# Feature products of 512 tokens run as two halves of 256, and one place for the memory key weights

## The chip, the cores and the metric

One core of one Trainium2 chip runs the whole kernel. The metric is the device time of one launch in microseconds (us), median of the runs shown; lower is better.

## What is computed

A decoder trunk of two layers over 512 tokens of width 1024, in float32. Each layer has three sub-layers, each between two RMS norms and added to the residual `x`:

```
x = x + rmsnorm(hybrid_mixer(rmsnorm(x)))            # one input projection; 8 heads of dilated causal
                                                      # attention, 4 mLSTM heads with a causal conv on
                                                      # q and k; one output projection
x = x + rmsnorm(memory_cross_attention(rmsnorm(x), mem))   # 4 heads, 256 memory tokens
x = x + rmsnorm(conv_ffn(rmsnorm(x)))                 # gated MLP of width 2816, conv of width 3
```

The change touches projections only: of the mixer, the conv inputs qm and km (`h @ w_in`, eight column blocks of 128) and attention's q and k (four and four blocks); of the cross attention, the queries (`h @ wq`) and the memory keys (`mem @ wk`).

## The kernel before, in words

**Products in three parts.** Every operand of a large product is split into a float32r high part and a float32r rest (`split`, L101: a copy on ScalarE, a subtraction on VectorE). `mm3` (L116) then issues three matmuls for one product: high by high, high by rest, rest by high. Weights come from DRAM as units of 128 x 1024 (512 KB), one `raw` tile each, and are split into a `whi` and a `wlo` tile. Such a tile is 1152 columns wide and the 1024 columns of weights start in it at an offset (`w_tiles`, L89): `offs` is the pair of offsets of `whi` and `wlo`, `WOFF` is (16, 48).

**Two kinds of product.** A *feature* product (`feat_gen`, L173) makes 128 features of all 512 tokens: the weights are stationary, the activations move. One unit is 8 blocks of the contraction by 3 matmuls, 24 matmuls of 512 columns, summed in one PSUM bank; after each block the generator yields. A *token* product (`tok_gen`, L203) has the activations stationary. `feat_halves` (L184) is a feature product that goes over tokens 0 to 255 for several units before tokens 256 to 511; it serves the first four query units of the cross attention and the first four units of the MLP, always at `WOFF`.

**Where `feat_gen` is used**, per layer: eight units U_Q and U_K of attention (L745, L746, at `WOFF`), eight conv units U_QM and U_KM (L722, each with its own pair out of `OFFS`), the last four of the eight query units of the cross attention (L1021, at `WOFF`), and `fill_k` (L423), which makes the memory keys: eight units per layer of 256 columns (the 256 memory tokens), at `OFFS[m]`; the first four of layer 1 are made earlier, in layer 0, at `WOFF`. That is 20 units of 512 columns per layer, 40 in all.

**The order of work.** TensorE's order is written out by the program: `run` (L154) takes one step of the main generator and then calls `tick` (L128), which lets side tasks that are due issue their matmuls. Due times come from a planned clock, `now`, which `mm` (L107) moves on for each matmul by a cost, and from waits in `PACE`. While the mixer's feature units run, the side tasks are the attention groups (scores, transposes of the probabilities `s`, products with the values) and the gates. So TensorE's stream there is a run of feature matmuls, some side matmuls, a run of feature matmuls, and so on; a run is three matmuls or a multiple of three. The other engines and the DMA queue take their instructions in the order that the tile framework plans, except in stretches marked as written by hand.

In the trace the tiles are named by what they are: `B` holds the normalised activations, `mem` the memory tokens, `pg` and `pa` are PSUM. A matmul reads out<-moving,stationary.

Of the kernel before, what the change touches and what calls it, by code (L numbers as in the profile page):

```python
# [21 lines left out]
NM = 256  # L22
# [6 lines left out]
U_QM, U_KM, U_VM, U_V, U_Q, U_K, U_OM = 0, 4, 8, 12, 16, 20, 24  # L29
U_WOUT, U_WQ, U_WK, U_WV, U_WO, U_UP, U_DOWN = 28, 36, 44, 52, 60, 68, 112  # L30
# [8 lines left out]
def trunk_kernel(ctx: ExitStack, tc: tile.TileContext, x4, memt, w, gw, gains, mcw, fcw, gb,  # L39
# [11 lines left out]
    def nm(s):  # L51
        uid[0] += 1
        return f"{s}_{uid[0]}"

    def pg():
        return ps.tile([128, 512], F32, tag="g", name=nm("pg"), bufs=4)
# [41 lines left out]
    def load_unit(l, i, offs=(0, 0)):  # L98
        return w_split(load_raw(l, i), offs)
# [7 lines left out]
    def mm(o, lhs, rhs, **kw):  # L107
        n = math.prod(o.shape[1:])
        now[0] += 0.0025 + (max(0.218, n / 600) if rhs.dtype == F32 else max(0.107, n / 2400))
        PE.matmul(o, lhs, rhs, **kw)  # L110
# [5 lines left out]
    def mm3(o, lh, ll, rh, rl, start, stop, **kw):  # L116
        mm(o, lh, rh, start=start, stop=False, **kw)
        mm(o, lh, rl, start=False, stop=False, **kw)
        mm(o, ll, rh, start=False, stop=stop, **kw)
# [53 lines left out]
    def feat_gen(l, u, act, done, n=512, w=None, offs=WOFF):  # L173
        hi, lo = w or load_unit(l, u, offs)
        acc = pg()
        for k in range(8):
            c = slice(128 * k, 128 * k + 128)
            rh, rl = act(k)
            mm3(acc[:, :n], hi[:, c], lo[:, c], rh, rl, k == 0, k == 7)
            if k == 7:  # L180
                done(acc)
            yield

    def feat_halves(l, units, act, dones, between, after=()):  # L184
        ws = [load_unit(l, u, WOFF) for u in units]
# [140 lines left out]
    def act_of(xn):  # L326
        def f(k):
            return xn[k // 4][:, k % 4, :], xn[2 + k // 4][:, k % 4, :]
        return f
# [86 lines left out]
    def dkv(l, which):  # L416
        if (l, which) not in kv_dram:
            kv_dram[l, which] = dr.tile([128, 2, 1024], F32, name=f"d{which}{l}")
        return kv_dram[l, which]

    OFFS = [(0, 0), (96, 0), (16, 48), (48, 48), (64, 0), (32, 64), (112, 16), (80, 112)]

    def fill_k(act, l, ms, offs=None):  # L423
        dst = dkv(l, "k")
        for m in ms:
            def done(acc):
                kf = pp.tile([128, NM], F32, tag="xg", name=nm("kf"), bufs=PACE["xg"])
                ACT.copy(kf, acc[:, :NM])
                SP.dma_start(dst[:, m // 4, NM * (m % 4):NM * (m % 4) + NM], kf)

            n = 0
            for _ in feat_gen(l, U_WK + m, act, done, NM, offs=offs or OFFS[m]):
                n += 1
                if n % 2 == 0:
                    yield
# [64 lines left out]
    def mixer(l, xn, pend):  # L500
        act = act_of(xn)
# [7 lines left out]
        def m16(tag):  # L509
            return mp.tile([128, 16], F32, tag=tag, name=nm(tag))  # L510
# [4 lines left out]
        cc, inter, floor, wt = m16("cc"), m16("inter"), m16("floor"), m16("wt")  # L515
# [196 lines left out]
        def conv_done(m):  # L712
            def f(acc):
                u = pp.tile([128, 512], F32, tag="xg", name=nm("u"), bufs=PACE["xg"])
                ACT.activation(u, acc, AF.Identity, bias=cw_t[:, m, 4:5], scale=cw_t[:, m, 3:4])
                for j in range(1, 4):
                    DVE.scalar_tensor_tensor(u[:, j:], acc[:, :512 - j], cw_t[:, m, 3 - j:4 - j], u[:, j:],
                                             ALU.mult, ALU.add)
                ACT.activation((qm if m < 4 else km)[:, m % 4, :], u, AF.Silu)
            return f  # L720

        conv = iter([feat_gen(l, U_QM + m, act, conv_done(m), offs=OFFS[m]) for m in range(8)])  # L722

        atasks = []
        for j in range(4):
            qas = [ap.tile([128, 512], F32R, tag=f"qa{i}", name=nm("qa"), bufs=2) for i in range(2)]
            khs = [ap.tile([128, 512], F32R, tag=f"kh{i}", name=nm("kh")) for i in range(2)]

            def q_done(acc, first=8 * (4 * l + j - 1)):
                until(lambda: live.get("S", 0) >= first)  # L730
                for hh in range(2):
                    a, b = hv[hh], hv[1 - hh]
                    ACT.activation(qas[hh][a], acc[a], AF.Copy, scale=0.125)
                    DVE.scalar_tensor_tensor(qas[hh][b], acc[a], 0.125, qas[hh][a].bitcast(F32),
                                             ALU.mult, ALU.subtract)

            def k_done(acc, first=8 * (4 * l + j)):
                until(lambda: live.get("S", 0) >= first)
                for hh in range(2):
                    a, b = hv[hh], hv[1 - hh]  # L740
                    ACT.copy(khs[hh][a], acc[a])
                    ACT.copy(khs[hh][b], acc[a])
                    DVE.tensor_sub(kls[hh][a], acc[a], khs[hh][a].bitcast(F32))

            run(feat_gen(l, U_Q + j, act, q_done))  # L745
            run(feat_gen(l, U_K + j, act, k_done))  # L746
            atasks.append(spawn(att_pair(j, qas, khs), PACE["aw"][l]))
            for _ in range(PACE["cv"][l][j]):
                run(next(conv))
# [514 lines left out]

    for l in range(L):
        mix_close, mixed = mixer(l, xn, pend)
        tail = Tail(l, G_POST_MIX, (l, G_PRE_MEM), PACE[f"nmem{l}"])

# [5 lines left out]
        pend = tail.tasks  # L1274
        xn = tail.xn
        run(fill_k(mem_tiles(pool_mem(tail.tp)), l, range(PACE["kf"][0] if l else 0, 8)))
        tail.close()
        es, tasks, o_t = cross(l, xn, pend)
# [11 lines left out]
        if l == 0:  # L1290
            run(fill_k(mem_tiles(lambda: tail.forms.wide(F32R)), 1, range(PACE["kf"][0]), WOFF))
            tail.forms.free = True
# [91 lines left out]
```

## Time and profile before

| | us |
|---|---|
| median of 3 runs (1556.23 to 1558.34) | 1556.98 |
| the profiled execution's own time | 1557.76 |
| its span, first to last instruction | 1555.9 |
| TensorE matmul busy | 1529.4 (98%) |
| VectorE busy | 1074.2 (69%) |
| ScalarE busy | 892.8 (57%) |

How to read it: busy time of a matmul record is its time from start to modelled end, and records of neighbouring matmuls overlap. What a matmul costs the stream is the step from its start to the start of the next one. In the timeline, neighbouring matmuls of one kind stand in one line with their number, so the step is read between the starts of lines.

### The profile page before, as it was taken

To read this page: it belongs to the slowest core of one execution; us is meant where nothing else is said; L and a number is where in the kernel's file an instruction comes from. 1 tells how busy PE (TensorE), PEld (TensorE's weight loads), DVE (VectorE), ACT (ScalarE), POOL (GpSimd) and SP (SyncE) were. 2 spreads that over 40 slices of the span, in tenths; PEclk is the share of its full clock that TensorE was granted. 3 is DMA by queue.
4 is the path that set the end of the run, shared out by engine and by line. 5 is a ranking of instruction groups with operands and counts; after the bars stand their busy time and mean duration, and the time that the engine had idled before them with its cause. 6 is when DMAs were issued, how large, how long until landed. Compare 5 with 4: busy or idle time off the path is not lost.

```text
span 1555.9 us, 24501 instructions
## 1 busy us (share of the span) xinstructions
PE 1529.4 (98%) x9480; PEld 1350.9 (87%) x9480; DVE 1074.2 (69%) x1808; ACT 892.8 (57%) x1578; POOL 355.7 (23%) x292
## 2 busy tenths in 40 slices
PE   7999999999999999999999999999999999999998
PEld 5788888898899999988887888888988899999886
DVE  5687646746588899963376876557565988998433
ACT  5687574545466666652256875745454666666321
POOL 0000110100026777700010001101000367773000
PEclk9999999999999999999999999999999999999999
DMA  5422245463242333342323222454521233332331
GB/s 179 129 81 79 79 134 166 128 198 110 80 138 82 109 109 109 111 131 98 108 89 115 89 68 82 141 156 142 179 73 35 104 104 112 111 115 91 128 101 55
DMA packets 55430, 173.13 MB, mean 111 GB/s; under 512 B 6801, under 2 KB 9617, under 8 KB 55314
## 3 DMA queue, kind: packets, MB, share of 16 engines
q1 hardware_dynamic: 55314, 171.57, 33.9%
q8 instruction: 74, 1.21, 0.3%
q14 instruction: 42, 0.34, 0.1%
HBM read 165.22 MB, written 6.33 MB: 110 GB/s over the span
## 4 chain that ended last, share of the span: by engine, by line
PE 70%; DVE 15%; ACT 4%; DMA 4%; issue 3%; POOL 2%; SPq 0%; POOLq 0%; DVEq 0%; ACTq 0%
PE pg L110 47%; PE pa L110 21%; DVE wlo L1137 4%; DVE u L1042 4%; PE pa L114 3%; DMA raw<-in_w_dram 2%; DVE wlo L103 2%; ACT u L1037 1%; ACT whi L102 1%; POOL sm L236 1%; DVE xg L262 1%; ACT junk L241 1%; DMA raw<-in_memt_dram 1%; DVE B L1056 1%; DVE x L375 1%
## 5 line engine op out<-in xcount | busy, mean ns | idle before, releaser
L110 PE MATMUL pg<-B,whi 128*128 128x256 f32 (+1 forms) x1800 | 412.4, 323 | 5.6 <-DVE u L1042 4.2
L103 DVE TENSOR_TENSOR wlo<-raw,whi 128x1024 fp32r<-128x1024 f32 x188 | 231.3, 1232 | 215.7 <-ACT whi L102 212.9
L102 ACT CAST whi<-raw 128x1024 fp32r<-128x1024 f32 x188 | 197.1, 1049 | 219.6 <-PE pg L110 136.5
L110 PEld LDWEIGHTS pg<-B,whi 128*128 128x128 f32 x1800 | 286.9, 188 | 25.7 <-ACT b L1131 2.3
L110 PE MATMUL pg<-whi,B 128*128 128x512 f32 x896 | 297.9, 399 | 0.0
L110 PE MATMUL pg<-B,wlo 128*128 128x256 f32 (+1 forms) x896 | 285.8, 319 | 0.0
L110 PEld LDWEIGHTS pg<-whi,B 128*128 128x128 f32 x896 | 168.8, 189 | 35.0 <-DVE B L103 1.3
L236 POOL TENSOR_TENSOR sm<-sm,mhalf 128x1 f32<-128x1 f32 x56 | 34.3, 612 | 719.4 <-DVE sm L361 542.7
L110 PEld LDWEIGHTS pg<-B,wlo 128*128 128x128 f32 x896 | 168.2, 188 | 14.2
L110 PE MATMUL pg<-wlo,B 128*128 128x512 f32 x448 | 175.3, 391 | 0.6 <-DVE sm L254 0.6
L110 PE MATMUL pa<-S,whi 128*128 128x256 f32 x960 | 168.5, 277 | 0.0
L1042 DVE SCALAR_TENSOR_TENSOR u<-pg,fcw,u 128x511 f32<-128x511 f32 (+1 forms) x176 | 131.3, 747 | 37.9 <-ACT u L1037 34.9
L110 PEld LDWEIGHTS pa<-S,whi 128*128 128x128 f32 x960 | 145.7, 189 | 0.0
L1137 DVE TENSOR_TENSOR wlo<-T,whi 128x1024 fp32r<-128x1024 f32 x80 | 131.7, 1646 | 2.5 <-ACT whi L1131 2.3
L110 PE MATMUL pa<-S,wlo 128*128 128x256 f32 x480 | 133.1, 277 | 0.0
L110 PE MATMUL pa<-whi,S 128*128 128x512 f32 x320 | 105.9, 390 | 0.0
L110 PE MATMUL pg<-whi,S 128*128 128x512 f32 x320 | 105.4, 390 | 0.0
L1037 ACT ACTIVATE u<-pg,fcw 128x512 f32<-128x512 f32 x88 | 68.6, 779 | 55.4 <-DVE pg L1185 28.6
L110 PEld LDWEIGHTS pg<-wlo,B 128*128 128x128 f32 x448 | 84.7, 189 | 15.9 <-DVE wlo L103 1.0
L1131 ACT CAST whi<-T 128x1024 fp32r<-128x1024 f32 x80 | 83.9, 1048 | 25.0 <-PE pg L110 10.9
L1137 POOL TENSOR_TENSOR b<-rg,b 128x512 fp32r<-128x512 f32 x40 | 74.0, 1851 | 100.7 <-ACT b L1131 100.7
L110 PEld LDWEIGHTS pa<-S,wlo 128*128 128x128 f32 x480 | 90.8, 189 | 0.0
(264 smaller groups left out, 2944.5 us busy)
## 6 DMA issues: line engine op xcount, KB each, us to landing
raw<-in_w_dram SPq DMA_DIRECT2D x228, 512.0 KB, 3.5
rg<-in_w_dram SPq DMA_DIRECT2D x40, 512.0 KB, 3.5
gain<-in_gains_dram SPq DMA_DIRECT2D x11, 512.0 KB, 4.3
raw<-in_memt_dram SPq DMA_DIRECT2D x20, 256.0 KB, 3.2
tb<-tb_d SPq DMA_DIRECT2D x16, 256.0 KB, 3.6
x<-in_x_dram SPq DMA_DIRECT2D x8, 256.0 KB, 5.4
e<-nmu_d SPq DMA_DIRECT2D x8, 256.0 KB, 3.6
dv<-vf SPq DMA_DIRECT2D x8, 256.0 KB, 4.2
```

What stands on the lines that cost most here:

```text
L102: ACT.copy(hi, src)
L103: DVE.tensor_sub(lo, src, hi.bitcast(F32))
L110: PE.matmul(o, lhs, rhs, **kw)
L114: PE.transpose(o, src, idn)
L236: POOL.tensor_tensor(r, v, mhalf[:, :1], ALU.pow)
L241: ACT.activation(junk[:, :src.shape[-1]], src, AF.Square, accum_out=s_)
L262: DVE.scalar_tensor_tensor(xg, xt[:, c], r, g[h], ALU.mult, ALU.mult)
L375: DVE.scalar_tensor_tensor(xs[t][:, cc], self.hg[hh, t], r, xs[t][:, cc], ALU.mult, ALU.add)
L1037: ACT.activation(u, acc, AF.Identity, bias=fcw_t[:, m, 3:4], scale=fcw_t[:, m, 2:3])
L1042: DVE.scalar_tensor_tensor(u[:, q:], acc[:, :512 - q], fcw_t[:, m, 2 - q:3 - q], u[:, q:], ALU.mult, ALU.add)
L1131: ACT.copy(ws[j, kind][0], source(j, kind))
L1137: sub(ws[j, kind][1], source(j, kind), ws[j, kind][0].bitcast(F32), ALU.subtract)
```

## The change

`feat_gen` works through the tokens 256 at a time: for 512 tokens the eight blocks of the contraction are issued for the first 256 columns and then again for the second 256, 48 matmuls of 256 columns in place of 24 of 512. It yields after every second block, so after six matmuls of 256 where it yielded after three of 512. For 256 columns (`fill_k`) the order is as it was. The table `OFFS` goes; the conv units take the default `WOFF`, and `fill_k` takes (32, 64) for all of its units that had an entry of the table.

```diff
     def feat_gen(l, u, act, done, n=512, w=None, offs=WOFF):
         hi, lo = w or load_unit(l, u, offs)
         acc = pg()
-        for k in range(8):
-            c = slice(128 * k, 128 * k + 128)
-            rh, rl = act(k)
-            mm3(acc[:, :n], hi[:, c], lo[:, c], rh, rl, k == 0, k == 7)
-            if k == 7:
-                done(acc)
-            yield
+        for c0 in range(0, n, 256):
+            cc = slice(c0, c0 + 256)
+            for k in range(8):
+                c = slice(128 * k, 128 * k + 128)
+                rh, rl = act(k)
+                mm3(acc[:, cc], hi[:, c], lo[:, c], rh[:, cc], rl[:, cc], k == 0, k == 7)
+                if k == 7 and c0 + 256 == n:
+                    done(acc)
+                if n == 256 or k % 2:
+                    yield
...
-    OFFS = [(0, 0), (96, 0), (16, 48), (48, 48), (64, 0), (32, 64), (112, 16), (80, 112)]
-
     def fill_k(act, l, ms, offs=None):
...
-            for _ in feat_gen(l, U_WK + m, act, done, NM, offs=offs or OFFS[m]):
+            for _ in feat_gen(l, U_WK + m, act, done, NM, offs=offs or (32, 64)):
...
-        conv = iter([feat_gen(l, U_QM + m, act, conv_done(m), offs=OFFS[m]) for m in range(8)])
+        conv = iter([feat_gen(l, U_QM + m, act, conv_done(m)) for m in range(8)])
```

## Rows read from the trace of the kernel before

**Rows 1.** The profile's page: span, busy time of TensorE, chain by engine

```profile
span 1555.9 us, 24501 instructions
...
PE 1529.4 (98%) x9480; PEld 1350.9 (87%) x9480; DVE 1074.2 (69%) x1808; ACT 892.8 (57%) x1578; POOL 355.7 (23%) x292
...
PE 70%; DVE 15%; ACT 4%; DMA 4%; issue 3%; POOL 2%; SPq 0%; POOLq 0%; DVEq 0%; ACTq 0%
```

**Rows 2.** Busy time in stretches, the mixers' feature units: stretch, length, busy by engine

```profile
core 0: us, PE busy (x) PEld busy (x) DVE busy (x) ACT busy (x) POOL busy (x), PEclk, DMA share, GB/s
...
45.00:166.00 121.00, 121.00 (x635) 100.40 (x634) 95.66 (x253) 90.81 (x178) 2.59 (x2) 1.00 0.29 92
...
822.20:944.00 121.80, 121.80 (x643) 101.34 (x642) 96.30 (x253) 93.31 (x180) 2.58 (x2) 1.00 0.27 87
```

**Rows 3.** Groups by shape, TensorE, 45 to 166 us: the feature matmuls

```profile
L110 PE MATMUL pg<-B,whi 128*128 128x512 f32 x256 | 83.5, 407 | 0.0
L110 PE MATMUL pg<-B,wlo 128*128 128x512 f32 x128 | 50.5, 395 | 0.0
```

**Rows 4.** Timeline, TensorE: start, length, what; 512 columns after transposes

```profile
91.69 0.71 PE L110 MATMUL pg<-B,whi 128*128 128x512 f32 x2
...
92.47 0.63 PE L110 MATMUL pg<-B,whi 128*128 128x512 f32 x2
...
93.17 0.62 PE L110 MATMUL pg<-B,whi 128*128 128x512 f32 x2
```

**Rows 5.** Timeline, TensorE: 256 columns after transposes (first MLP units)

```profile
454.54 0.48 PE L110 MATMUL pg<-B,whi 128*128 128x256 f32 x2
...
455.33 0.40 PE L110 MATMUL pg<-B,whi 128*128 128x256 f32 x2
...
456.03 0.39 PE L110 MATMUL pg<-B,whi 128*128 128x256 f32 x2
...
456.71 0.39 PE L110 MATMUL pg<-B,whi 128*128 128x256 f32 x2
```

**Rows 6.** Timeline, TensorE: 512 columns after score matmuls of 384 columns

```profile
77.83 0.63 PE L110 MATMUL pg<-B,whi 128*128 128x512 f32 x2
...
78.52 0.63 PE L110 MATMUL pg<-B,whi 128*128 128x512 f32 x2
```

**Rows 7.** Timeline, TensorE: 256 columns after token matmuls of 512 columns

```profile
1204.68 0.40 PE L110 MATMUL pg<-B,whi 128*128 128x256 f32 x2
...
1205.38 0.39 PE L110 MATMUL pg<-B,whi 128*128 128x256 f32 x2
...
1206.06 0.39 PE L110 MATMUL pg<-B,whi 128*128 128x256 f32 x2
```

**Rows 8.** Timeline, TensorE: 512 columns after score matmuls of 128 columns

```profile
75.79 0.67 PE L110 MATMUL pg<-B,whi 128*128 128x512 f32 x2
...
76.53 0.63 PE L110 MATMUL pg<-B,whi 128*128 128x512 f32 x2
```

**Rows 9.** Timeline, TensorE: a long run of 512 columns, from a unit's first rest weights

```profile
57.56 0.40 PE L110 MATMUL pg<-B,wlo 128*128 128x512 f32 x1
57.80 0.62 PE L110 MATMUL pg<-B,whi 128*128 128x512 f32 x2
...
58.48 0.62 PE L110 MATMUL pg<-B,whi 128*128 128x512 f32 x2
```

**Rows 10.** Timeline, TensorE: starts of memory key units 2, 3, 5, 6 and 7, layer 0

```profile
303.28 0.40 PE L110 MATMUL pg<-mem,whi 128*128 128x256 f32 x2
...
306.14 0.41 PE L110 MATMUL pg<-mem,whi 128*128 128x256 f32 x2
...
313.21 0.40 PE L110 MATMUL pg<-mem,whi 128*128 128x256 f32 x2
...
315.95 0.39 PE L110 MATMUL pg<-mem,whi 128*128 128x256 f32 x2
...
318.79 0.40 PE L110 MATMUL pg<-mem,whi 128*128 128x256 f32 x2
```

**Rows 11.** Timeline, TensorE: transposes within the memory keys, idle before them in brackets

```profile
308.05 0.63 PE L114 MATMUL pa<-ident,xg 128*128 128x128 f32 x4 [0.31 <-DVE xg L262]
```

**Rows 12.** Timeline, VectorE: the rest weights of the unit of rows 9

```profile
52.63 1.23 DVE L103 TENSOR_TENSOR wlo<-raw,whi 128x1024 fp32r<-128x1024 f32 x1 [1.07 <-ACT whi L102]
```

## The prediction

> **What bounds the kernel now.** I read the page first: TensorE is busy for 1529.4 of 1555.9 us and carries 70% of the chain that ended last [rows 1]. Then the table of stretches, for the two places where most of the changed units run: in 45 to 166 us TensorE is busy for 121.00 of 121.00, in layer 1 for 121.80 of 121.80 [rows 2]. No engine and no transfer is waited for there, so what counts is the step from one matmul's start to the next one's. Busy time does not tell it: the groups by shape give 407 ns for one of the 256 + 128 feature matmuls of that stretch [rows 3], but their records overlap. So I went to the timeline and read starts. A product of three matmuls of 512 columns (a triple, one yield of the generator) steps by 0.70 us in the middle of a run [rows 4, 6]; six matmuls of 256 columns (the same work after the change) step by 0.70 at first and by 0.68 later on [rows 5, 7].
>
> That "later on" is what the forecast hangs on. A run of halves comes to 0.68 only after six to twelve matmuls: 0.79, 0.70, 0.68 after transposes [rows 5], 0.70, 0.68 after wide matmuls [rows 7]. A run of wholes gets there too, but far later: 0.68 shows after more than 30 matmuls without a break [rows 9]. In the mixer the runs are short. I counted them in the timeline of 45 to 166 us: 384 feature matmuls in 67 runs. 30 runs begin after transposes or other small matmuls (23 of one triple, 3 of two, 3 of three, one of 17); 17 begin after side matmuls of 128 columns (5, 9 and 3 of one, two and three triples); 20 after wide ones (8 of one, 6 of two, 4 of three, one of four, one of five). More than half are over after one triple.
>
> **The change part by part.** *Halves in the mixers*, 16 units per layer, 128 triples. Price of a triple, halves against whole:
> - First triple after transposes: 0.79 against 0.78 [rows 4, 5]; the rows are rounded to 0.01, I take +0.015 each, 30 times: +0.45 us.
> - First triple after 128-column matmuls: whole 0.74 [rows 8]; no row shows halves there. Bounds are the row after transposes (+0.015) and the row after wide matmuls (about 0); it is nearer to the first, since both start late (0.74 and 0.78 against 0.69). I take +0.01, 17 times: +0.15.
> - First triple after wide matmuls: 0.70 [rows 7] against 0.69 [rows 6], +0.005, 20 times: +0.1.
> - Second triple of the two late kinds: 0.70 against 0.70 [rows 4, 5], nothing, 19 times.
> - All later ones, and the second after wide matmuls: 0.68 [rows 5, 7] against 0.69 to 0.70 [rows 4, 6], -0.015. That is 21 after wide matmuls, 3 of the 128-column kind, and 18 of the transposes' kind, of which the last five or so gain nothing as the long run has settled by itself [rows 9]: 37 times -0.015, -0.55.
>
> Sum: about +0.2 per mixer, +0.4 for both. The bounds: all halves at 0.68 from the first on would give -1.5 per mixer, none ever at 0.68 would give +2.3 (below).
>
> *Halves of the queries*, four units per layer in the cross attention: 64 triples in 13 runs of two to eight triples, all after wide matmuls. 51 of them are not the first of their run: 51 times -0.015, -0.7.
>
> *One offset for the memory keys.* In layer 0 the unit with (32, 64) runs from 313.21 to 315.95, 2.74 us; its neighbour with (112, 16) takes 2.84, and unit 2, at (16, 48), 2.86 [rows 10]. Ten units get (32, 64) that had another pair. Five have no transposes in between: 5 x 0.11. In five the runs are broken and only the later part gains, half of it: 5 x 0.05. Together -0.8. The row, then, says that the place of the stationary tile counts. The Trainium skill ("TensorE: Matmul & The Clock Gate", section "Step-by-step: what each phase is for") says that weight loads and the moving operand have independent read ports, so that loading the next weights takes no read bandwidth from the running matmul; by it the place would count for nothing and this -0.8 would be 0.
>
> *The conv units' offsets.* All sixteen go to (16, 48). For 512 columns the rows of these units look like those of q and k at (16, 48); no cost. For halves (16, 48) with tile `B` is what rows 5 and 7 show.
>
> *What a wait takes back.* In layer 0's memory keys TensorE waits 0.31 us for a norm on VectorE [rows 11]; the units before it get about 0.25 shorter, and that wait longer by as much. A little more goes the same way in the cross attention: +0.3 in all.
>
> *Edits at nothing.* DMAs, splits, PSUM tiles and evacuations are the same in number, and an evacuation still comes after a unit's last matmul. The rest weights are needed after two halves, not two wholes, 0.23 us earlier; VectorE has them ready at 53.86 for a use at 57.56 [rows 9, 12], and without that cover TensorE would wait 0.2 us at most per unit. Yields come after the same work. The planned clock books 0.219 for two halves where it booked 0.216, 0.08 us per unit, so some side tasks come one yield (0.7 us) earlier among the feature matmuls; with no idle time in the stretch [rows 2] most producers must be well ahead, and I allow 1 us either way for this and for a new order on the other engines.
>
> Sum: +0.4 - 0.7 - 0.8 + 0.3 = -0.8 us. Against the profiled execution's own 1557.76 (span 1555.9) that is 1557.0; that execution lies 0.8 above the median of the runs, 1556.98, so I forecast **1556.2**. A measurement of this kernel tells about 0.2%, 3.1 us, from no change.
>
> **Rivals.** *Settled at once.* If the halves in the mixer run at 0.68 from their second triple on at the latest and lose nothing at the start, every triple gains up to 0.015 save the long run's last: -1.5 per mixer, -3.0 - 0.7 - 0.8 + 0.3 = -4.2, **1552.8**. For it: after wide matmuls the second triple is at 0.68 already [rows 7]. Against: after transposes it is not [rows 5], and those are the most frequent starts.
>
> *Never settled* (slower). The rate after a break has a cause that the mixer renews, and halves stay at what unit 2 of the memory keys shows with the same offsets (16, 48) and another moving tile: 2.86 / 4 = 0.715 for six [rows 10] against 0.695. That is +0.018 for 128 triples, +2.3 per mixer: +4.6 - 0.7 - 0.8 + 0.3 = +3.4, **1560.4**. It decides from about 0.713 for six halves, taken over all. For it: side matmuls break the runs 67 times per mixer. Against: with `B` as moving tile every long run in the trace settled.
>
> *The offset does nothing.* Unit 5 is fast for another reason and the memory keys gain nothing; the waits take back less: +0.4 - 0.7 + 0.1 = -0.2, **1556.8**. For it speaks the rule of the read ports. Against: unit 6, right behind unit 5 in the same quiet stretch, is slow [rows 10].
>
> **How the numbers follow.** Forecast 0.55, own range 1555 to 1558.5 (1 us for the order, and bounds of the 128-column starts); settled at once 0.17; never settled 0.16; offset does nothing 0.12. Faster by over 0.2% (below 1553.9): 0.15 of the second case, some of the first: 0.21. Slower (above 1560.1): most of the third and a little of the first: 0.19. Within: 0.60. The range reaches to both outer cases, 1552.8 to 1560.4, since leaving out both would leave out a third.
>
> **What would show it.** Right: in the mixers' feature units, timeline steps of about 0.79, 0.70, 0.68 for groups of six halves after transposes, and the two stretches (121.0 and 121.8 us) within 1 us of before; the four query units of a layer shorter by 0.35; each quiet memory key unit at 2.74; no idle time of TensorE in the mixers' stretch. Wrong: steps of 0.68 right after transposes (settled at once) or 0.71 throughout (never settled); memory key units still at 2.84; or TensorE idle before transposes of `s`, which would say that the new order cost more than the steps.

## The result and the profile after

The changed kernel takes **1565.43 us** (median of 4 runs, 1562.81 to 1568.26) against 1556.61 for the kernel before on the same chip (4 runs, 1556.00 to 1558.34): a ratio of **1.0059**, 95% interval 1.0047 to 1.0072. It is slower by 0.6%, outside the forecast's range of 1555 to 1558.5 and above its slowest rival, 1560.4. Measured again later it took 1563.80 (5 runs, 1561.74 to 1567.82) against 1555.57, a ratio of 1.0055 [1.0042, 1.0067].

The profiled execution is the fastest of the four: 1562.81 us with a span of 1561.0, against 1557.76 and 1555.9 before. So the two traces show 5.1 of the 8.8 us between the medians. The page, where [rows 1] stood before:

```profile
span 1561.0 us, 26418 instructions
...
PE 1527.9 (98%) x10440; PEld 1394.2 (89%) x10440; DVE 1075.5 (69%) x1808; ACT 894.1 (57%) x1578; POOL 355.4 (23%) x292
...
PE 69%; DVE 16%; ACT 5%; DMA 4%; issue 3%; POOL 2%; SPq 0%; POOLq 0%; DVEq 0%; ACTq 0%
```

TensorE is busy 1.5 us less than before, in a span that is 5.1 longer. The page alone doesn't say where; starts of the same instruction in both traces do. The table gives the time between such starts (the last gate matmul, the first `ones,sq`, the first `mem,whi`, the last `mem,whi`, the first `ph,v` of each layer), read from the timelines. The last `mem,whi` comes 0.2 to 0.6 us ahead of the first query unit; it stands for that unit's start in this table and wherever the stretch to the heads is given below:

| stretch | before | after | difference |
|---|---|---|---|
| start to the mixer's feature units, layer 0 | 45.2 | 45.6 | +0.4 |
| feature units of mixer 0, to its norm | 127.8 | 129.9 | **+2.1** |
| memory keys, layer 0 | 24.6 | 23.5 | -1.15 |
| first query unit to the heads, layer 0 | 50.9 | 53.5 | **+2.6** |
| heads to the mixer's feature units, layer 1 | 449.8 | 449.0 | -0.8 |
| feature units of mixer 1, to its norm | 127.8 | 130.4 | **+2.6** |
| memory keys, layer 1 | 12.8 | 12.6 | -0.2 |
| first query unit to the heads, layer 1 | 50.6 | 50.0 | -0.7 |
| heads of layer 1 to the end | 419.8 | 419.9 | +0.1 |

(The stretches left out, between a mixer's norm and the memory keys, differ by under 0.1.) Three stretches lose 7.3 us. The mixers have idle time now. The busy time of the same lengths as in [rows 2], shifted by 0.6 and 3.1 us, about as late as its units start:

```profile
core 0: us, PE busy (x) PEld busy (x) DVE busy (x) ACT busy (x) POOL busy (x), PEclk, DMA share, GB/s
45.60:166.60 121.00, 119.20 (x1001) 116.72 (x1000) 94.47 (x251) 89.53 (x176) 2.58 (x2) 1.00 0.30 91
825.30:947.10 121.80, 120.20 (x1005) 117.73 (x1004) 95.55 (x251) 90.90 (x177) 2.59 (x2) 1.00 0.30 88
```

TensorE idles 121.00 - 119.20 = 1.8 us and 121.80 - 120.20 = 1.6 us, where [rows 2] had none. Its waits in the first of these stretches (engine, line, what it waited for: us in total, times, longest); the same view of the kernel before is empty:

```profile
engine line waited for: us in total, times, longest us
PE pa L110 <- DVE pl L103: 1.3, 3, 0.6
PE pa L110 <- ACT ph L102: 0.3, 1, 0.3
PE pa L114 <- DVE s L660: 0.2, 1, 0.2
```

These are side tasks of the attention, not the feature tiles that the change touches. Two of the waits in the timeline of TensorE, and what VectorE did before the second one:

```profile
97.23 0.28 PE L110 MATMUL pa<-pl,B 128*128 128x128 f32 x1
97.80 0.39 PE L110 MATMUL pa<-ph,B 128*128 128x256 f32 x1 [0.30 <-ACT ph L102]
...
121.56 0.39 PE L110 MATMUL pa<-pl,B 128*128 128x256 f32 x1 [0.60 <-DVE pl L103]
```

```profile
119.53 0.74 DVE L718 SCALAR_TENSOR_TENSOR u<-pg,mcw,u 128x509 f32<-128x509 f32 x1
120.30 0.69 DVE L703 TENSOR_TENSOR ao<-pa,lo 64x512 f32<-64x512 f32 x1
121.02 0.16 DVE L659 RECIPROCAL sm<-sm 128x1 f32<-128x1 f32 x1
121.09 0.41 DVE L103 TENSOR_TENSOR pl<-pa,ph 128x256 fp32r<-128x256 f32 x1
```

VectorE is not idle: `pl` stands behind the conv's sums `u` and an evacuation. The same product and its `pl` before:

```profile
121.06 0.28 PE L110 MATMUL pa<-pl,B 128*128 128x256 f32 x1
```

```profile
119.36 0.42 DVE L103 TENSOR_TENSOR pl<-pa,ph 128x256 fp32r<-128x256 f32 x1
```

There `pl` was ready 121.06 - 119.36 - 0.42 = 1.28 us ahead. Counted from the last gate matmul (45.20 before, 45.59 after), TensorE now comes to this product 0.5 us earlier (75.37 us, its wait taken off, against 75.86), and VectorE, whose own order has changed too, makes `pl` 1.3 us later (75.50 against 74.16). Together that is 1.8 us: the margin is gone and some 0.55 us are missing, the wait of 0.60.

The feature matmuls themselves do what the forecast said. A run of halves after transposes, to be read against [rows 4, 5]:

```profile
94.80 0.48 PE L110 MATMUL pg<-B,whi 128*128 128x256 f32 x2
...
95.58 0.39 PE L110 MATMUL pg<-B,whi 128*128 128x256 f32 x2
...
96.26 0.39 PE L110 MATMUL pg<-B,whi 128*128 128x256 f32 x2
...
96.94 0.28 PE L110 MATMUL pa<-ph,B 128*128 128x256 f32 x1
```

Six halves take 0.78, 0.68 and 0.68 us (the last line begins the next product). The memory keys, where [rows 10] stood, start at even distances of 2.72 us, and the transposes between them no longer wait [rows 11]:

```profile
309.80 0.60 PE L114 MATMUL pa<-ident,xg 128*128 128x128 f32 x4
...
314.82 0.39 PE L110 MATMUL pg<-mem,whi 128*128 128x256 f32 x2
...
317.54 0.39 PE L110 MATMUL pg<-mem,whi 128*128 128x256 f32 x2
...
320.26 0.39 PE L110 MATMUL pg<-mem,whi 128*128 128x256 f32 x2
```

The third loss is in the cross attention of layer 0. TensorE's waits from 323 to 377 us; before, in the same place, the only one was 1.0 us for `p`:

```profile
PE pa L114 <- DVE p L966: 2.8, 1, 2.8
PE pg L110 <- DVE wlo L103: 0.5, 1, 0.5
```

VectorE's timeline there, with the wait that it causes on TensorE:

```profile
364.26 1.23 DVE L103 TENSOR_TENSOR wlo<-raw,whi 128x1024 fp32r<-128x1024 f32 x1 [2.78 <-ACT whi L102]
...
365.73 0.42 DVE L961 TENSOR_REDUCE sm<-pa 128x1 f32<-128x256 f32 x1
366.98 1.22 DVE L103 TENSOR_TENSOR wlo<-raw,whi 128x1024 fp32r<-128x1024 f32 x1 [0.83 <-ACT whi L102]
368.12 0.15 DVE L965 RECIPROCAL sm<-sm 128x1 f32<-128x1 f32 x1
368.20 0.40 DVE L103 TENSOR_TENSOR pl<-pa,ph 128x256 fp32r<-128x256 f32 x1
368.52 1.28 DVE L1004 SCALAR_TENSOR_TENSOR ql<-pg,qh 128x512 fp32r<-128x512 f32 x2
369.71 0.34 DVE L966 TENSOR_SCALAR p<-p,sm 128x256 f32<-128x256 f32 x1
```

```profile
367.12 0.28 PE L110 MATMUL pg<-B,wlo 128*128 128x256 f32 x1
370.20 0.41 PE L114 MATMUL pa<-ident,p 128*128 128x128 f32 x2 [2.81 <-DVE p L966]
```

In this order `p`, which TensorE waits for, stands behind two splits of weights, for each of which VectorE idles (2.78 and 0.83 us) until ScalarE has made the weights' large part, and behind both evacuations of `ql`. It stood behind both `ql` before, too:

```profile
364.01 1.23 DVE L103 TENSOR_TENSOR wlo<-raw,whi 128x1024 fp32r<-128x1024 f32 x1 [0.64 <-ACT whi L102]
365.15 0.15 DVE L964 RECIPROCAL sm<-sm 128x1 f32<-128x1 f32 x1
365.24 1.29 DVE L1003 SCALAR_TENSOR_TENSOR ql<-pg,qh 128x512 fp32r<-128x512 f32 x2
366.44 0.34 DVE L965 TENSOR_SCALAR p<-p,sm 128x256 f32<-128x256 f32 x1
```

From the start of the split to `p` it was 2.43 us and is 2.73 now, by one `pl` more. The larger difference in this trace is the split itself: it starts 44.0 us after the query unit's first matmul (366.98 - 322.98), before 42.4 (364.01 - 321.65).

### The profile page after: what moved, and what is told of

Same layout as the page of the kernel before. It is cut to its first block, busy times and chain, and to the rows that moved or that the text cites. A ratio compares the mean times of both kernels' runs of the same rounds, so it can differ in the third digit from the quotient of the medians.

```text
span 1561.0 us, 26418 instructions
## 1 busy us (share of the span) xinstructions
PE 1527.9 (98%) x10440; PEld 1394.2 (89%) x10440; DVE 1075.5 (69%) x1808; ACT 894.1 (57%) x1578; POOL 355.4 (23%) x292
## 4 chain that ended last, share of the span: by engine, by line
PE 69%; DVE 16%; ACT 5%; DMA 4%; issue 3%; POOL 2%; SPq 0%; POOLq 0%; DVEq 0%; ACTq 0%
PE pg L110 45%; PE pa L110 21%; DVE wlo L1138 4%; DVE u L1043 4%; DMA raw<-in_w_dram 3%; PE pa L114 2%; DVE wlo L103 2%; ACT whi L102 1%; ACT u L1038 1%; DVE u L718 1%; DMA raw<-in_memt_dram 1%; DVE xg L265 1%; DVE B L1057 1%; POOL sm L239 1%; ACT junk L244 1%
## 5 line engine op out<-in xcount | busy, mean ns | idle before, releaser
L110 PE MATMUL pg<-B,whi 128*128 128x256 f32 (+1 forms) x2440 | 439.0, 281 | 5.5 <-DVE u L1043 4.0
L110 PEld LDWEIGHTS pg<-B,whi 128*128 128x128 f32 x2440 | 371.7, 188 | 9.1 <-ACT b L1132 2.3
L110 PE MATMUL pg<-B,wlo 128*128 128x256 f32 x1216 | 337.4, 277 | 0.5 <-DVE wlo L103 0.5
L110 PEld LDWEIGHTS pg<-B,wlo 128*128 128x128 f32 x1216 | 228.5, 188 | 1.0 <-DVE wlo L103 0.9
L239 POOL TENSOR_TENSOR sm<-sm,mhalf 128x1 f32<-128x1 f32 x56 | 34.3, 612 | 718.8 <-DVE sm L364 542.4
```

Of the source, the lines that this page charges most:

```text
L239: POOL.tensor_tensor(r, v, mhalf[:, :1], ALU.pow)
```

## The experiments

All are variants of the two kernels. The planned clock `now[0]` books time for each matmul, and a side task goes on at the first yield at which its due time has passed; the bookings decide the order in which TensorE gets the instructions, and take no time themselves.

**The halves in the old order** (`e1_order_kept`): the changed kernel, but each triple's worth of halves is booked as the three wholes were.

```diff
+                at = now[0]
...
+                if n == 512:
+                    now[0] = at + 1.5 * (0.0025 + 512 / 2400)
```

> The changed kernel, but the planned clock books for two halves what it booked for one whole (0.2158 us), so TensorE's order of units and side tasks is that of the kernel before; halves and offsets stay. Theory A (the cost is the new order: side tasks come one or two yields too early and TensorE waits): idle time of TensorE in the mixers' feature stretches falls from 2.2 and 2.0 us to about 0.4 each (the old waits), the wait in layer 0's cross attention from 2.8 to about 1 us, and the time is 0.5 to 2.5 us below the kernel before. Theory B (the halves themselves cost: steps, weights needed earlier): idle time stays and the time is 5 to 9 us above before.

Measured: 1556.01 us (12 runs), ratio 1.0000 [0.9991, 1.0008]. The loss is gone with the order alone, all halves and offsets kept; a gain, as theory A had it, does not show. The stretch of mixer 0 is 0.2 us shorter than before, that of mixer 1 0.3 longer, and from the first query unit of layer 0 to the heads it takes 49.0 us, 1.9 less than before. One wait is left in the first mixer:

```profile
PE pa L114 <- DVE s L663: 0.2, 1, 0.2
```

**The new order with the old matmuls** (`e2_booked_only`): the kernel before, with a triple of wholes booked as six halves.

```diff
+            at = now[0]
...
+            if n == 512:
+                now[0] = at + 6 * 0.1095
```

> The kernel before with wholes and its old offsets; only the planned clock books 0.219 us where it booked 0.2158, so the order of the side tasks is that of the changed kernel. Theory A: slower than before by 4 to 8 us without a single half, with the waits of the changed kernel (about 1.8 and 1.6 us more idle in the two mixers, 1.5 to 2 us more in the cross attention of layer 0). Theory B: no difference to before.

Measured: 1561.67 us (5 runs), ratio 1.0036 [1.0023, 1.0049]. A number in the planner, and no instruction more or less, costs 5 us. The stretches of the mixers are 2.3 us longer each, and TensorE idles 1.6 us in each, nearly as long as in the changed kernel, if partly before other matmuls. Layer 0's cross attention loses nothing, where theory A had 1.5 to 2 us. The waits in the first mixer:

```profile
PE pa L114 <- DVE s L662: 0.8, 1, 0.8
PE pa L110 <- DVE pl L103: 0.7, 2, 0.3
```

**The offsets alone** (`e3_offsets_only`): the kernel before, with the conv units at (16, 48) and the memory keys at (32, 64).

```diff
-... offs=offs or OFFS[m]):
+... offs=offs or (32, 64)):
...
-        conv = iter([feat_gen(l, U_QM + m, act, conv_done(m), offs=OFFS[m]) for m in range(8)])
+        conv = iter([feat_gen(l, U_QM + m, act, conv_done(m)) for m in range(8)])
```

> The kernel before with wholes; only the offsets are those of the change: memory keys at (32, 64), conv units at (16, 48). Both theories: memory key stretch of layer 0 about 0.7 to 1.1 us shorter, of layer 1 0.2, the rest as before; time 0.5 to 1.3 us below before. If the offset did nothing: the same time, units at 2.84 us.

Measured: 1556.18 us (11 runs), ratio 0.9999 [0.9990, 1.0007]. The memory keys are shorter by 1.15 us in layer 0 and by 0.2 in layer 1, as in the changed kernel (how much of it the offset makes, `e10_old_keys` tells); the time does not show it, and a gain of that size lies within the interval.

**The halves alone** (`e4_halves_only`): the changed kernel with the old table of offsets for keys and conv units.

```diff
+    OFFS = [(0, 0), (96, 0), (16, 48), (48, 48), (64, 0), (32, 64), (112, 16), (80, 112)]
...
-            for _ in feat_gen(l, U_WK + m, act, done, NM, offs=offs or (32, 64)):
+            for _ in feat_gen(l, U_WK + m, act, done, NM, offs=offs or OFFS[m]):
```

> The changed kernel with the old table of offsets: halves and the new order, not the new offsets. Both theories: about 1 us above the changed kernel, so 6 to 10 us above before; memory key units at 2.84 us again. If the conv units' offsets matter for halves (a run settles to 0.68 us for six at (16, 48) only), the mixers' feature steps get longer too, by up to 2 us per mixer.

Measured: 1562.21 us (5 runs), ratio 1.0041 [1.0029, 1.0053]. That is 5.7 us above before, a little less than the 6 to 10 that both theories gave, and not above the changed kernel. The halves, with what they book, bring the loss with them; the offsets don't. The quiet memory key units are at 2.83 to 2.86 us again where they had another pair, and the mixers are 0.4 to 0.5 us longer than in the changed kernel.

**The changed kernel again** (`e5_changed_again`), beside the next three on one chip:

> The changed kernel itself, beside the others on one chip. Theory A: it lies where the kernel with halves and the old offsets lay (5 to 6 us above before) or up to 1.3 us below that; the 8.8 us of its first four runs were in part a less lucky set of runs, its long wait in layer 0's cross attention (2.8 us) varies from run to run with the landing of weights. If halves and the new offsets together cost something of their own: 8 to 9 us above before again, with that wait at 2.5 us or more.

Measured: 1563.80 us, ratio 1.0055 [1.0042, 1.0067], as told above. That is 8.2 us above before: more than theory A's 6, so in these runs the changed kernel costs something beyond the new order. Its trace has the same waits; for `p` in layer 0 it is 2.46 us.

**Booked less** (`e6_booked_less`): is 0.216 per whole merely the right side, or an optimum? The wholes of the kernel before, booked at 0.2126 (the diff is to `e2_booked_only`).

```diff
-                now[0] = at + 6 * 0.1095
+                now[0] = at + 6 * 0.1063
```

> The kernel before, wholes and old offsets, with the planned clock booking 0.2126 us per whole in place of 0.2158, as far below as the change is above. Theory A1 (side tasks come too early): later side tasks wait less, the idle time in the mixers stays at 0.4 us, time within 2 us of before. Theory A2 (the order is a narrow optimum, any shift by a yield costs): 3 us or more above before, with side tasks that follow one another too closely and new idle time.

Measured: 1575.18 us (4 runs), ratio 1.0125 [1.0109, 1.0140]. 1.5% less on the clock costs 19.6 us (against 1555.57): the mixers' stretches are longer by 9.1 and 10.0 us. So it is no drift with one good direction. Part of it is TensorE's clock: at the end of each mixer's stretch the granted clock is 0.84 in the mean of 172.0 to 182.8 us and 0.71 in 955.0 to 966.9, so 3.5 and 6.9 us at the lower level of 1.2 GHz, which cost about half as much. The waits of its first mixer:

```profile
PE pa L114 <- DVE s L662: 2.2, 1, 2.2
PE pa L110 <- DVE pl L103: 2.0, 4, 0.8
PE pa L110 <- ACT ph L102: 1.5, 2, 1.0
```

**Where the order counts** (`e7_booked_mixer`): as `e2_booked_only`, but in the mixers only.

```diff
-            if n == 512:
+            if n == 512 and u < U_WQ:
```

> The kernel before with 0.219 booked for the mixers' units alone (q, k, conv); the queries of the cross attention are booked as before. Theory A: the mixers carry the loss, so 4 to 5.5 us above before, idle time of 2 us in each mixer; the rest is as before. Rival: the cross attention's order carries a good part, then 2.5 us or less.

Measured: 1561.44 us (5 runs), ratio 1.0037 [1.0025, 1.0050], the same as with the booking everywhere. With wholes, all of the loss is the mixers'.

**The halves alone in the old order** (`e8_halves_order_kept`): `e4_halves_only` with the booking of `e1_order_kept`.

> Halves alone: the old offsets, and the planned clock books as before, so TensorE's order is the one before. Price of the halves by themselves. By the forecast's terms: mixers +0.2 us each, queries -0.35 each, no idle time over 0.6 us in a mixer; time -0.7 to +1 us against before. If weights that are needed 0.23 us earlier or the doubled number of weight loads cost something: 2 us or more above before.

Measured: 1556.48 us (11 runs), ratio 1.0006 [0.9997, 1.0014]. The mixers' stretches are 0.4 and 0.9 us longer than before, 0.6 us per mixer more than with the conv units at (16, 48) in `e1_order_kept`: for halves that offset counts; for wholes, in `e3_offsets_only`, it changed a mixer by 0.1 to 0.15.

What was left open: the changed kernel lies 2 to 4 us above the new order alone, and loses 2.6 us in layer 0's cross attention, where `e2_booked_only` loses nothing (50.1 us for the stretch).

**Whole queries** (`e9_whole_queries`): the changed kernel with the query units as wholes, booked as halves.

```diff
-        for c0 in range(0, n, 256):
-            cc = slice(c0, c0 + 256)
+        step = 512 if n == 512 and u >= U_WQ else 256
+        for c0 in range(0, n, step):
+            cc = slice(c0, c0 + step)
...
+                if step == 512:
+                    now[0] = at + 6 * 0.1095
```

> The changed kernel, but the query units stay wholes, booked as two halves, so that TensorE issues its units and side tasks in the order of the changed kernel. What is open is why the changed kernel lies 2 to 4 us above the kernel with the new order alone (1561.7): in its layer-0 cross attention TensorE waits 2.5 to 2.8 us at 369 to 370 us for p from VectorE, where the kernel before waits 0.96. Theory Q (the halves of the queries bring TensorE to that product earlier, or keep it waiting): the wait falls to under 1.2 us and the median to 1560.5 to 1562.5. Theory K (the memory keys, 1.15 us shorter, bring TensorE early to a stage that is fed by its weights, and the wait only swallows what they gain): the wait stays at 2 us or more and the median at 1562.5 to 1565.

Measured: 1563.13 us (5 runs), ratio 1.0037 [1.0024, 1.0050]. The stretch to the heads falls to 51.6 us and the wait to 1.61, between what the two theories gave, while the median is where theory K had it; VectorE's order there is not the changed kernel's either. Inconclusive.

**Old keys** (`e10_old_keys`): the changed kernel with the memory keys at their old offsets.

```diff
-            for _ in feat_gen(l, U_WK + m, act, done, NM, offs=offs or (32, 64)):
+            for _ in feat_gen(l, U_WK + m, act, done, NM, offs=offs or OFFS[m]):
```

> The changed kernel, but the memory keys lie at their old offsets. Theory K (see the run before): the memory keys of layer 0 take about 1.1 us more, the wait for p in the layer-0 cross attention falls from 2.5 to 2.8 us to about 1.5, and the median stays where the changed kernel is, 1563 to 1565.5. Theory Q: the wait stays at 2.2 us or more and the time rises by what the keys lose, 0.8 to 1.4 us. Theory S (the spread is chance: the changed kernel's extra 2 to 4 us over the new order alone come from waits at the start of the feed-forward stages and the clock that follows, which vary from run to run): 1561 to 1564 with either wait.

Measured: 1561.13 us (12 runs, 1558.43 to 1564.77), ratio 1.0031 [1.0021, 1.0041]. The wait for `p` stays at 2.2 us, so theory K falls: the shorter keys don't make that wait. The keys of layer 0 are 0.6 us longer than in the changed kernel, not 1.1: so 0.6 is what the offset is worth there. The other 0.5 of the 1.15 us lies in unit 3, where TensorE waits for a norm in the kernel before [rows 11]. That unit takes 4.24 us there, 3.73 here with the same offsets, 3.72 to 3.73 in `e2_booked_only`, `e4_halves_only`, `e6_booked_less` and `e7_booked_mixer`, and 3.82 in `e8_halves_order_kept`. That the time is lower than the changed kernel's, with more work on TensorE, no theory named but the one of chance; the two profiled spans, 1561.8 and 1561.2, don't show it, and it stays open. The trace of this run shows one more price of such a wait. Busy time in three stretches, the wait in the second one (the granted clock is the third number from the end):

```profile
355.00:368.00 13.00, 11.31 (x99) 11.11 (x98) 8.27 (x15) 6.64 (x12) 0.00 (x0) 1.00 0.57 169
368.00:373.00 5.00, 4.46 (x26) 4.49 (x27) 3.30 (x9) 2.55 (x7) 0.00 (x0) 0.66 0.28 98
373.00:385.00 12.00, 11.76 (x75) 10.36 (x75) 7.50 (x18) 5.49 (x14) 0.00 (x0) 1.00 0.25 83
```

TensorE idled 2.2 us up to 368.5; then the granted clock is 0.66 in the mean of these 5 us: 3.4 us of them at the lower level of 1.2 GHz, since 5 x (1 - 0.66) / 0.5 = 3.4. `e5_changed_again` has 0.66 in the same place. The changed kernel's first profile has 1.00 there, though its wait was longer.

**The gains alone** (`e11_halves_in_queries`): the mixers in wholes, the queries in halves booked as wholes, all offsets as in the changed kernel.

```diff
-        for c0 in range(0, n, 256):
-            cc = slice(c0, c0 + 256)
+        step = 512 if n == 512 and u < U_WQ else 256
+        for c0 in range(0, n, step):
+            cc = slice(c0, c0 + step)
```

> The parts of the change that the forecast priced as gains, in the old order: the mixers as before (wholes, conv units at their old... offsets as the changed kernel has them, (16, 48)), the query units in halves booked as wholes, the memory keys at (32, 64). The forecast's own sum for this is -0.7 for the queries, -0.8 for the keys, +0.3 for waits: -1.2 us, 1555.3. If the layer-0 cross attention is fed by its weights and swallows what TensorE saves ahead of it, layer 0 gives nothing and 0.3 to 0.6 us of layer 1 are left: 1555.9 to 1556.3. Neither is far enough from 1556.5 for the time to tell by itself, so the stretches of the trace decide: the start of the heads in layer 0 earlier by 1.5 us, and the end of that cross attention earlier by 1.2 (the forecast) or by under 0.3 (swallowed).

Measured: 1555.56 us (12 runs), ratio 0.9995 [0.9986, 1.0005]. The heads of layer 0 start 2.5 us earlier than before, and the stage behind that cross attention starts 2.8 earlier: not swallowed, and more than the forecast's 1.2. Of these, 1.15 us come from the keys (0.5 of them the wait for the norm) and 1.5 from the stretch to the heads. The profiled span is 3.7 us shorter; the median moves by 0.1, within the interval. By the medians it cannot be told from the kernel before.

**VectorE's order in the cross attention** (`e12_queries_booked`): the changed kernel with the booking of `e1_order_kept` for the queries alone.

```diff
+                at = now[0]
...
+                if n == 512 and u >= U_WQ:
+                    now[0] = at + 1.5 * (0.0025 + 512 / 2400)
```

> The changed kernel, but the query units' halves are booked on the planned clock as the wholes were; the mixers keep the new booking. VectorE's order then differs from the changed kernel's in one place of each layer's cross attention: in layer 0 the scaling of p stands ahead of the two evacuations of ql (0.6 us each), where the changed kernel has it behind them. Theory V (what the layer-0 cross attention loses in the changed kernel is p standing behind ql, by the new booking alone): the wait for p falls from 2.5 to 2.8 us to 1.5 or less, the stretch from the first query unit to the heads, 53.5 us in the changed kernel, comes to 50 to 52, and the median to 1560.5 to 1562: only the mixers' loss, 4.6 us, is left, with about 1 us taken off by the keys. Theory W (TensorE is held there by the weights' transfers, whatever VectorE's order): the stretch stays at 52.8 us or more and the median at 1562.5 to 1565. In both cases the mixers stay 2.0 and 2.6 us longer than before.

Measured: 1560.25 us (10 runs), ratio 1.0026 [1.0016, 1.0035]: theory V's side, the stretch and the median a little below what it gave. The stretch to the heads takes 49.8 us and TensorE has no wait from 321 to 372 us, while the mixers stay 2.0 and 2.5 us longer than before. VectorE's timeline has `p` ahead of `ql`:

```profile
363.57 1.23 DVE L103 TENSOR_TENSOR wlo<-raw,whi 128x1024 fp32r<-128x1024 f32 x1 [1.29 <-ACT whi L102]
364.71 0.16 DVE L968 RECIPROCAL sm<-sm 128x1 f32<-128x1 f32 x1
364.78 0.41 DVE L103 TENSOR_TENSOR pl<-pa,ph 128x256 fp32r<-128x256 f32 x1
365.10 0.34 DVE L969 TENSOR_SCALAR p<-p,sm 128x256 f32<-128x256 f32 x1
...
365.70 1.28 DVE L1007 SCALAR_TENSOR_TENSOR ql<-pg,qh 128x512 fp32r<-128x512 f32 x2
```

So what the queries book is the cause of this loss. By which order it works is less clear than theory V has it, since the booking moves TensorE's order as well: these transposes of `p` follow 177 feature matmuls' worth of the stage here and before, and 174 in the changed kernel, one yield less. Three traces in which the split starts about equally late tell the two apart (us; starts are counted from the query unit's first matmul, and TensorE is free when all ahead of the transposes is done):

| trace | split starts at | split to `p` | TensorE free at | TensorE's wait |
|---|---|---|---|---|
| `e12_queries_booked` | 42.1 | 1.53 | 44.1 | none |
| before | 42.4 | 2.43 | 44.3 | 0.96 |
| `e5_changed_again` | 42.6 | 2.73 | 43.4 | 2.46 |

`p` ahead of both `ql` is worth 0.9 us against the kernel before. Of the 1.5 us that the changed kernel waits longer than the kernel before, 0.9 come from TensorE, which is there earlier, 0.3 from one more `pl` ahead of `p` and 0.3 from the split. In the changed kernel's first trace TensorE is free at 44.4 us, 0.5 of it a wait for a `wlo`, and the split at 44.0 makes most of the difference. And `p` ahead of `ql` is no guarantee: `e8_halves_order_kept` has that order and still waits 1.66 us, behind a split that starts at 43.4. Why the split comes when it does (it waits for the weights' transfer and for ScalarE) was not taken apart.

## Why the prediction was wrong

**The step that failed** is the last of the edits costed at nothing: "The planned clock books 0.219 for two halves where it booked 0.216 [...] so some side tasks come one yield (0.7 us) earlier among the feature matmuls; with no idle time in the stretch [rows 2] most producers must be well ahead, and I allow 1 us either way for this and for a new order on the other engines." That side tasks would move was seen rightly: the first transpose of `s` comes after 81 feature matmuls' worth instead of 84, the first products `ph,B` after 96 instead of 99. But they move by up to two yields and both ways: of the 48 products `ph,B` of mixer 0, 14 come earlier, 12 of them by two yields, and 6 later. The price was wrong. Measured, the new order costs 5.1 us with nothing else changed (`e2_booked_only`, 1561.67 against 1556.52), all of it in the mixers as far as the runs tell (`e7_booked_mixer`), and 3.9 us with the cross attention's order kept (`e12_queries_booked`, 1560.25 against 1556.32).

The inference was the fault. That TensorE has no idle time says that no producer is late; it doesn't say by how much each is early. The trace had the margin in it: for the product at 121.06 `pl` was ready 1.28 us ahead, under two yields. And a new order of TensorE's brings a new one on VectorE, which took 1.3 us of that margin where TensorE took 0.5. Which of the two orders costs more over a whole mixer no run separates. Each mixer then has 1.6 to 1.8 us of idle time and 1.0 and 1.3 us more between the starts of side matmuls (34.3 to 35.4 us in mixer 0, summed over the timeline): transposes of `s` 6.3 to 6.8 us, the products `ph,B` and `pl,B` 10.4 to 10.9. The second part was not taken apart further.

**Halves in the mixers**, forecast +0.2 us each: about right in the order that the forecast counted its runs in. Summed from start to start, without idle time, the 768 feature matmuls of a mixer take 92.13 and 92.54 us after, against 92.90 and 92.82 for the 384 before; in the old order (`e1_order_kept`) 92.58 and 92.98, which is -0.3 and +0.2. In that order the first triples after transposes take 0.79 to 0.80 us in the mean against 0.78 before, and the third and later ones of a run mostly 0.68 against 0.69 to 0.70, as the working had it. Rival "never settled" would have shown +2.3 and is out; "settled at once" (-1.5) is out too. After the transposes shown above the second triple is at 0.68, not at 0.70 as in [rows 5].

**Halves of the queries**, forecast -0.35 us per layer. In layer 1 the stretch is 0.67 shorter with them and 0.26 with whole queries (`e9_whole_queries`): -0.4, as forecast. In layer 0 the sum did not hold, since the stretch goes by when the split and `p` come: +2.6 us in the changed kernel, and where halves run in the old order and `p` stands ahead of `ql`, -1.1 to -1.9 in three traces and +0.2 in `e8_halves_order_kept`.

**One offset for the memory keys**, forecast -0.8: right in sign, place and size. Against the same kernel with the old offsets (`e10_old_keys`) the keys are 0.63 us shorter in layer 0 and 0.23 in layer 1, together -0.86. The quiet units gain 0.06 to 0.14 us each (unit 2 takes 2.72, in `e10_old_keys` and before 2.86), the broken ones 0 to 0.05. The traces of before and after differ by more, -1.15 - 0.22 = -1.4, because the wait for the norm [rows 11], which was to grow by 0.25, went away; it is missing with the old offsets too, so the offset did not take it, and what did stays open. Rival "the offset does nothing" is out by the same comparison. The Trainium skill ("TensorE: Matmul & The Clock Gate", section "Step-by-step: what each phase is for") says that weight loads and the moving operand have separate read ports, and the prediction drew from it that the place would not count. Here 24 matmuls of the same shape take 2.72 or 2.86 us by the place of the stationary tile, so what was drawn from it does not hold; whether the ports have part in that no run here shows.

**The waits that take back 0.3 us** were looked for behind what the change makes faster. The wait that came is one for `p`, which the list of what stays "the same in number" did not cover: the number of VectorE's instructions is the same, their order is not. The forecast named "a new order on the other engines" and priced it with the same 1 us.

**What would show it wrong** did, if mostly one step further on: the prediction had "TensorE idle before transposes of `s`, which would say that the new order cost more than the steps". In mixer 0 of the changed kernel 0.2 us of the idle time lie before transposes of `s`, the other 1.6 are waits for `pl` and `ph`. The sign stood there without a price, and so had no chance of its own; the one rival on the slower side, at 1560.4, was about the steps.

**Slips in the working** that change nothing in this account: the queries have 14 runs and not 13, one of a single triple. Of the ten key units six have no transposes in between and not five; by the working's own terms that gives -0.9. For "never settled", 0.715 against 0.695 is 0.020 and not 0.018 per triple, so +2.6 per mixer. The -1.5 of "settled at once" lets first triples gain as well; by its condition, 0.68 from the second triple on and nothing lost before, 19 second triples at -0.02 and 37 later ones at -0.015 give -0.9.

The sum by the traces: mixers +4.7, layer 0's queries +2.6, layer 1's -0.7, keys -1.4, all other stretches -0.2; together +5.1, the difference of the spans. How far one trace can be trusted shows in the last stretch, from the heads of layer 1 to the end, in which no edited matmul lies: it takes 419.3 to 420.1 us in ten traces and 421.3 to 421.7 in the other four (`e1_order_kept`, `e2_booked_only`, `e7_booked_mixer`, `e8_halves_order_kept`). The further 3.7 us between the medians are not in these two traces: the profiled execution is the changed kernel's fastest and the one before was above its median. The other three executions had a granted clock of 0.996, 0.996 and 0.995 in the mean against 0.999. By an estimate from these figures, 0.003 to 0.004 of 1561 us is 4.7 to 6.2 us of full clock, about the 1.4 to 5.5 us by which they are longer. `e5_changed_again` shows one way to it, the lower level behind the wait for `p`, worth about half of its 3.4 us; where the rest of it lay in those three executions no trace shows.

## What to carry to other kernels

Where a planner's clock sets the order of the instructions, a change of what an operation books is a change of the order, and it has to be priced like a moved wait: for each side task, the time from its operand's end to its use in the trace, against the shift in yields and against what the new order does to the engine that makes the operand. If a change is about something else, keep the bookings (`e1_order_kept` took three lines), and tune them apart. Worked out from the program, every booking from 0.2140 to 0.2174 per whole gives the old order and 0.2178 the new one; of such values only 0.2126, 0.2158 and 0.2190 were run, and the change booked 0.2190.

A full engine shows no margins. Before relying on "no idle time", read for some of its operands how long they had been ready; and of every in-order queue that feeds it read the order, not only the count.

## What the runs showed that was not expected

- An edit of one number without any instruction added moved the time by +0.4% in one direction and by +1.25% in the other (`e2_booked_only`, `e6_booked_less`).
- The place of the stationary tile matters more to 256-column matmuls than to 512-column ones: with the conv units at the old offsets a mixer's feature matmuls take 93.4 and 93.7 us in halves (`e8_halves_order_kept`) and 92.6 and 93.0 at (16, 48); wholes take 92.9 and 93.0 at either.
- Behind an idle time of TensorE of 2.2 to 2.5 us in layer 0's cross attention the granted clock fell to its lower level for 3.4 us in two traces (0.66 in the mean of 368 to 373 us); behind one of 2.8 us in another it did not. Every trace, the kernel before included, has such a fall in layer 1's feed-forward stage, where TensorE waits 2.0 us: the granted clock is 0.84 in the mean of 1229 to 1250 us before and 0.92 in the changed kernel, so 6.7 and 3.4 us at the lower level.
